# A transformer layer on one core: the side work of a pair moved behind the low parts of its activations

## The chip, the cores and the metric

The kernel runs on one core of a Trainium2 chip. The metric is the device time of one execution in microseconds (us), as the median of several runs. The engines are PE (TensorE, matmul) with its weight loads (PEld), DVE (VectorE), ACT (ScalarE), POOL (GpSimd) and SP (SyncE), which here issues all the DMAs.

## The reference, cut to what matters

One encoder layer is applied to 512 + 1024 tokens of width 1024, in float32:

```python
h = h + concat([attention(q, k, v), pooling(u)]) @ w_out
m = rmsnorm(h, norm_mlp_g)
h = h + square(relu(m @ w_up)) @ w_down          # the stage of this change; D_FF = 4096
gate = sigmoid(rmsnorm(h, norm_ple_g) @ w_ple_gate)
h = h + gate * (p_i @ w_ple_proj)
return rmsnorm(h, final_norm_g)
```

## The kernel before, in words

Every float32 operand of a matmul is split into a high part (a cast on ACT) and a low part (a subtraction on DVE or POOL); a product is three matmuls, high x high, high x low, low x high (`three`). The 1536 tokens are three chunks `c` of 512. A residual chunk `hT[c]` is four blocks of 128 x 2 x 512, each in one of 49 slots of one shared pool.

The stages follow each other: input projection (to about 190 us), attention with the output projection (to 579 us), the MLP (579 to 1625 us), the gated embedding and the last norm. PE, ACT, DVE and POOL execute in the order in which the program names the instructions. SP's order is chosen by a scheduler among what is ready; `load` adds that a load isn't put ahead of the last PE instruction named before it.

**The MLP.** For each chunk there are 16 pairs (`Pair(c, g)`), each of 256 of the 4096 hidden units. `run` computes the 2 x 2 blocks of a pair by seven products (Strassen's scheme) of 12 matmuls with 256 columns, in the order 1, 6, 2, 5, 7, 3, 4. Products 1 and 2 add up in one PSUM bank (`px`), 5 and 3 in another (`pz`), 7 and 4 in a third (`pq`); 6 has `py`. Between them stand the four down blocks of the pair before (`between(i)` calls `before.down(i)`): 12 matmuls with 512 columns into `pd`, whose sum DVE adds to `hT[c][i]` (L837). The order on PE is 1, down 0, 6, 2, down 1, 5, 7, down 2, 3, 4, down 3.

The tail of a pair makes its activations: ACT takes relu of c1 and of c2, the square as high part (L876, L882) and the exact square (L877, L883), and DVE the low parts (L886) into `r`. Down 0 of the next turn needs them.

**Side work.** After each product, `after(i)` issues one step of each of these: `feeding` (the sums and splits of the next pair's w_up, L786 to L804, and the load of w_up after that, `wur`), `splits` (w_down of this pair, L816 and L817), `raising` (L662, at the start of a chunk), and `step()`, one step of the queue `chores`. Chores are generators: `make_m` builds the normed inputs `mo_d` of a chunk, `spill` stores a residual chunk, `invert` and `finishing` belong to a chunk's end. `after(3)` and `after(4)` stand ahead of the low parts, so their instructions come first on DVE and ACT.

**The norm of the MLP.** The residual is multiplied with a per-token row w before the chunk's pairs add to it (`raise_h`: 8 operations on DVE). The end of `make_m(c)` computes w into `acc[:, 1]` (L646), stores it in `w_d[c]` (L647), and `load_ms(c)` loads it at the chunk's first pair.

**Start of the stage.** `heads_out(p)` gives eight pieces of the output projection for each 256 tokens; p = 5 are the last tokens of chunk 2. When they are through, `spill(2)` joins the chores, waits 16 steps and stores the four blocks of chunk 2 (L708). Meanwhile the 14 halves of `mo` for chunk 0 are loaded, then `h` of chunk 0, and `wur` of pair 1 by the fourth step of `feeding`.

Of the kernel before, what the change touches and what calls it, by code (L numbers as in the profile page):

```python
# [20 lines left out]
KD = D // P  # L21
# [14 lines left out]
def encoder_layer(ctx, tc, xT, xn, xr, pT, w1, w2, w_pool, w_out, w_up, w_down, w_gate, w_proj,  # L36
# [558 lines left out]
    def make_m(c, et, el):  # L595

        A, B = slice(0, HF), slice(HF, CH)
        acc = slot([P, 2, CH], F32, f"sqm{c}")  # L600

        def squares_of(b, m):
            for i in range(2):
                sq = slot([P, 2, CH], F32, f"sqm{c}{b}{i}")
                for h in range(2):
                    out = sq[:, h] if b + i + h else acc[:, 0]
                    yield ((lambda i=i, h=h, out=out: sc.activation(out, m[i][:, h], AF.Square)),
                           (lambda out=out, first=b + i + h == 0: None if first else
                            et.tensor_tensor(acc[:, 0], acc[:, 0], out, op=ALU.add)))

        for b in range(2):
            m = [slot([P, 2, CH], F32, f"m{c}_{2 * i + b}") for i in range(2)]
            for i in range(2):
                load(m[i], h_d[c][2 * i + b])
            yield from wait(5)
            yield from lagged(squares_of(b, m))
            for i in range(2):
                for h in range(2):
                    k = 2 * (2 * i + b) + h
                    sc.activation(m[i][:, h], m[i][:, h], AF.Copy, scale=gmlp_sb[:, k:k + 1])  # L620
                yield
            tt = [slot([P, 2, 2, HF], F32, f"t{c}_{b}{i}") for i in range(2)]
            t1, t2, t3, t4 = (tt[i // 2][:, i % 2] for i in range(4))
            b11, b12, b21, b22 = m[0][:, :, A], m[0][:, :, B], m[1][:, :, A], m[1][:, :, B]
            for o, x, y in ((t1, b12, b11), (t2, b22, t1), (t3, b22, b12), (t4, b21, t2)):
                et.tensor_tensor(o, x, y, op=ALU.subtract)
                yield

            def pairs():
                for i, x in ((1, b11), (6, t2), (2, b21), (5, t1), (7, t3), (3, b22), (4, t4)):  # L630
                    out = slot([P, 2, 2, HF], F32R, f"mm{c}_{i}{b}")

                    def low_part(i=i, x=x, out=out):
                        el.tensor_tensor(out[:, 1], x, as32(out[:, 0]), op=ALU.subtract)
                        for j in range(2):
                            sy.dma_start(mo_d[c][i][j][:, 2 * b:2 * b + 2], as32(out[:, j]))
                    yield (lambda x=x, out=out: sc.copy(out[:, 0], x)), low_part
            yield from lagged(pairs())
        sh = slot([P, 2, CH], F32R, f"sh{c}")
        sc.copy(sh[:, 0], acc[:, 0])  # L640
        el.tensor_tensor(sh[:, 1], acc[:, 0], as32(sh[:, 0]), op=ALU.subtract)
        yield from wait(7)
        bc = tp_ps(f"w{c}")
        for i in range(2):
            pe.matmul(bc, ones_sb, sh[:, i], start=i == 0, stop=i == 1)
        ve.tensor_scalar(acc[:, 1], bc, 1.0 / D, EPS, op0=ALU.mult, op1=ALU.add)  # L646
        sy.dma_start(w_d[c], acc[:, 1])  # L647

    def load_mo(c, i):
        MO[c, i] = [slot([P, 4, HF], F32R, f"mo{c}_{i}{j}") for j in range(2)]  # L650
# [52 lines left out]
    away = set()  # L703

    def spill(c):
        yield from wait(16 if c == 2 else 0)
        for a in range(4):
            sy.dma_start(h_d[c][a], hT[c][a])  # L708
        away.add(c)
        yield  # L710
# [30 lines left out]
    def heads_out(p):  # L741

        c, sl = p // 2, slice(p % 2 * 2 * P, (p % 2 + 1) * 2 * P)

        def piece(d):
            def go():
                assert c not in away
                h = hT[c][d // 2][:, d % 2, sl]
                po = (ps("pp", f"po{p}{d}") if prompt[0] else ps("s", f"po{p}{d}") if ending[0] and (p == 4 or d % 2)
                      else acc_ps("acc", f"po{p}{d}"))[:, 0:2 * P]  # L750
                for k in range(4):
                    ws = [w[:, d * P:(d + 1) * P] for w in WO[k]]
                    for i, (w_, x_) in enumerate(three(ws, [x[:, k, :] for x in cat[p]])):
                        pe.matmul(po, w_, x_, start=k == 0 and i == 0, stop=k == 3 and i == 2)
                ve.tensor_tensor(h, po, h, op=ALU.add)
                if d == KD - 1 and p % 2:
                    chores.append(spill(c))
                    if c == 0:
                        chores.append(make_m(0, gp, gp))
            return go  # L760
        return [piece(d) for d in range(KD)]


    class Pair:
# [62 lines left out]

        def down(self, a):
            pd = ps("d", f"pd{self.id}{a}")
            for e in range(2):  # L830
                d = 2 * a + e
                for f in range(2):
                    ws_ = [w[:, d * P:(d + 1) * P] for w in self.wd[f]]
                    for i, (w_, x_) in enumerate(three(ws_, [self.r[f][:, 0], self.r[f][:, 1]])):
                        pe.matmul(pd[:, e * CH:(e + 1) * CH], w_, x_, start=f == 0 and i == 0, stop=f == 1 and i == 2)
            h = hT[self.c][a]
            ve.tensor_tensor(h, pd.rearrange("p (a b) -> p a b", a=2), h, op=ALU.add)  # L837

        def run(self, between, after):

            A, B = slice(0, HF), slice(HF, CH)
            u = slot([P, 4, HF], F32, f"u{self.id}")
            t, u2, u4 = u[:, 0], u[:, 1], u[:, 2]
            c = slot([P, 2, CH], F32, f"c{self.id}")
            c1, c2 = c[:, 0], c[:, 1]
            self.r = [slot([P, 2, CH], F32R, f"r{self.id}{i}") for i in range(2)]

            def bank(tag, nm):
                return (tp_ps(f"{nm}{self.id}") if tag == "tp" else ps(tag, f"{nm}{self.id}"))[:, 0:HF]

            x = bank("tp", "px")
            self.product(1, x)
            sc.copy(t, x)
            after(1)
            between(0)
            y = bank("u", "py")
            self.product(6, y)
            ve.tensor_tensor(u2, y, t, op=ALU.add)
            after(6)
            self.product(2, x, False)  # L860
            sc.activation(c1[:, A], x, AF.Relu)
            after(2)
            between(1)
            z = bank("tp", "pz")
            self.product(5, z)
            ve.tensor_tensor(u4, z, u2, op=ALU.add)
            after(5)
            q = bank("u", "pq")
            self.product(7, q)
            ve.tensor_tensor(c2[:, B], q, u4, op=ALU.add)  # L870
            after(7)
            between(2)
            self.product(3, z, False)
            ve.tensor_tensor(c1[:, B], z, u2, op=ALU.add)
            sc.activation(c1[:, B], c1[:, B], AF.Relu)
            sc.activation(self.r[0][:, 0], c1, AF.Square)  # L876
            sc.activation(c1, c1, AF.Square)  # L877
            after(3)
            self.product(4, q, False)
            ve.tensor_tensor(c2[:, A], q, u2, op=ALU.add)  # L880
            sc.activation(c2, c2, AF.Relu)
            sc.activation(self.r[1][:, 0], c2, AF.Square)  # L882
            sc.activation(c2, c2, AF.Square)  # L883
            after(4)
            for i, x in enumerate((c1, c2)):
                ve.tensor_tensor(self.r[i][:, 1], x, as32(self.r[i][:, 0]), op=ALU.subtract)  # L886
            between(3)

    NG = NF // 2
    pairs = [Pair(c, g) for c in range(3) for g in range(NG)]  # L890

    def stream():

        for n, pr in enumerate(pairs):
            for i, _ in enumerate(pr.feed()):
                if i == 3 and n + 1 < len(pairs):
                    pairs[n + 1].load_up()
                yield
    feeding = stream()
# [167 lines left out]

    pairs[0].load_down()
    load_mo(0, ORDER[5]), load_mo(0, ORDER[6])
    for a in range(4):  # L1070
        load_h(0, a, h_d[0][a])
    while fill:
# [107 lines left out]
    for n, pair in enumerate(pairs):  # L1180
        c, g = pair.c, pair.g
        raising = None
        if g == 0:
            if c:
                for a in range(4):
                    load_h(c, a, h_d[c][a])
            load_ms(c)
            raising = raise_h(c)
        if g == 1:
            chores.append(invert(c))  # L1190
# [10 lines left out]
            if i == 1 and n + 1 < len(pairs):  # L1201
                pairs[n + 1].load_down()

        def after(i):
            next(feeding, None)
            next(splits, None)
            if raising:
                next(raising, None)
            if g == NG - 1 and c < 2:
                load_mo(c + 1, i)  # L1210
            if n == len(pairs) - 1:
                if i == 1:
                    chores.append(first_weights())
                if i in (5, 7, 3, 4):
                    load_in(0, (5, 7, 3, 4).index(i))
            step()

        pair.run(between, after)
        for _ in splits:
            pass  # L1220
        for _ in raising or ():
# [175 lines left out]
```

## Time and profile before

| what | us |
|---|---|
| median of 3 runs (1812.99 to 1815.73) | 1815.48 |
| the profiled execution, its own time | 1813.31 |
| its span | 1811.5 |
| PE busy | 1759.7 |
| DVE busy | 1260.0 |
| POOL busy | 1053.7 |
| ACT busy | 939.7 |

The granted clock of TensorE was 0.995 over the span; 256.84 MB were moved by DMA. In the rows of the profile a busy share is that of a span or window, a wait is put down to what ended it ("x <- y"), and L49 is the line of every matmul, so groups are told apart by the tiles' names: `pd` is a down block, `px`, `py`, `pz`, `pq` are products. Rows of a timeline give start, duration, engine, line, operation, and in brackets the idle time just before.

### The profile page before, as it was taken

The page shows a single profiled execution, that of the slowest core. Times are in us where ns is not written, and L with a number is a line of the kernel's source. Part 1 is how long each engine was busy: PE and PEld are TensorE (multiplying, and loading weights), DVE is VectorE, ACT ScalarE, POOL GpSimd, SP SyncE. Part 2 cuts the span into 40 slices and gives each one's busy share as a digit, 9 for nine tenths or more (in the row PEclk, how much of TensorE's full clock was granted, in tenths as well). Part 3 has the DMA queues.
Part 4 walks back from the last instruction along what each step waited for, and adds up shares of the span by engine and source line. Part 5 has one row for each costly group of instructions (what it writes and reads, how often), then busy time and mean ns, then how long its engine had stood idle before and what let it go on. Part 6 is the DMA issues. An engine that isn't in the chain of part 4 may idle for free.

```text
span 1811.5 us, 28604 instructions
## 1 busy us (share of the span) xinstructions
PE 1759.7 (97%) x10540; PEld 1537.1 (85%) x10540; DVE 1260.0 (70%) x1843; ACT 939.7 (52%) x1854; POOL 1053.7 (58%) x923
## 2 busy tenths in 40 slices
PE   9999899999999799999999999999999999999997
PEld 7888777888868798988888889889898999888887
DVE  5677865888894677865568877876776556665655
ACT  6434455768794455655445545554455444443332
POOL 3474774535674567676656776785577666543121
PEclk9999999999999899999999999999999999999998
DMA  6333545120519335343364442556443323272102
GB/s 248 114 123 105 216 165 185 36 94 13 206 46 367 139 122 198 121 177 100 136 265 157 163 151 96 195 185 235 179 157 100 110 94 99 89 262 70 59 12 82
DMA packets 83883, 256.84 MB, mean 142 GB/s; under 512 B 9888, under 2 KB 16416, under 8 KB 83744
## 3 DMA queue, kind: packets, MB, share of 16 engines
q1 hardware_dynamic: 83744, 255.02, 39.7%
q8 instruction: 83, 1.36, 0.3%
q14 instruction: 56, 0.46, 0.1%
HBM read 195.74 MB, written 59.24 MB: 141 GB/s over the span
## 4 chain that ended last, share of the span: by engine, by line
PE 78%; DVE 7%; ACT 5%; DMA 3%; issue 3%; POOL 1%; POOLq 0%; DVEq 0%; ACTq 0%; SPq 0%
PE pd L49 25%; PE z L49 7%; PE px L49 6%; PE pz L49 6%; PE pq L49 6%; PE pg L49 6%; PE py L49 4%; PE pp L49 3%; PE o L49 3%; PE tp L53 3%; PE po L49 3%; PE S L49 3%; PE pj L49 1%; DMA wur<-in_w_up_dram 1%; DVE r L886 1%
## 5 line engine op out<-in xcount | busy, mean ns | idle before, releaser
L49 PE MATMUL pd<-r,wd 128*128 128x512 f32 x2304 | 568.5, 395 | 10.8 <-DVE r L886 10.6
L49 PEld LDWEIGHTS pd<-r,wd 128*128 128x128 f32 x2304 | 419.5, 188 | 100.3 <-DVE r L886 16.1
L787 POOL TENSOR_TENSOR w<-ws,w 128x512 fp32r<-128x512 f32 x192 | 272.5, 1423 | 217.9 <-ACT w L786 206.8
L787 POOL TENSOR_TENSOR w<-wur,w 128x512 fp32r<-128x512 f32 x144 | 212.8, 1489 | 135.4 <-ACT w L786 134.4
L837 DVE TENSOR_TENSOR h<-pd,h 128x1024 f32<-128x1024 f32 x192 | 233.5, 1216 | 76.6 <-PE pd L49 76.5
L786 ACT CAST w<-ws 128x512 fp32r<-128x512 f32 x192 | 118.5, 617 | 271.1 <-DVE ws L795 241.1
L461 POOL TENSOR_SCALAR pr<-pr,rr 128x512 f32<-128x512 f32 x160 | 111.2, 705 | 134.7 <-DVE rr L456 66.8
L49 PE MATMUL z<-w,x 128*128 128x512 f32 (+1 forms) x864 | 175.7, 359 | 0.9 <-DVE w L160 0.5
L49 PEld LDWEIGHTS pz<-mo,w 128*128 128x128 f32 x1152 | 150.7, 190 | 19.3 <-issue 11.2
L49 PEld LDWEIGHTS z<-w,x 128*128 128x128 f32 x864 | 142.9, 189 | 28.0 <-ACT w L159 2.1
L49 PE MATMUL pz<-mo,w 128*128 128x256 f32 x1152 | 153.6, 283 | 10.2 <-issue 10.2
L817 DVE TENSOR_TENSOR wd<-wdr,wd 128x512 fp32r<-128x512 f32 x96 | 102.8, 1071 | 83.1 <-ACT wd L816 76.6
L49 PE MATMUL pq<-mo,w 128*128 128x256 f32 x1152 | 153.7, 283 | 1.0 <-issue 1.0
L49 PE MATMUL px<-mo,w 128*128 128x256 f32 x1152 | 152.2, 281 | 0.0
L49 PEld LDWEIGHTS px<-mo,w 128*128 128x128 f32 x1152 | 146.5, 189 | 4.0
L49 PEld LDWEIGHTS pq<-mo,w 128*128 128x128 f32 x1152 | 144.7, 191 | 1.4 <-issue 1.3
L49 PE MATMUL pg<-hg,wg 128*128 128x512 f32 (+1 forms) x768 | 141.0, 338 | 0.2
L472 ACT CAST pt<-tp 128x512 fp32r<-128x512 f32 x160 | 88.0, 591 | 88.5 <-PE tp L53 86.8
L49 PEld LDWEIGHTS pg<-hg,wg 128*128 128x128 f32 x768 | 118.6, 188 | 17.8 <-DVE hg L1128 1.0
L817 POOL TENSOR_TENSOR wd<-wdr,wd 128x512 fp32r<-128x512 f32 x96 | 131.8, 1373 | 2.6 <-DMA w_d<-sqm 2.6
L886 DVE TENSOR_TENSOR r<-c,r 128x512 fp32r<-128x512 f32 x96 | 74.7, 783 | 74.1 <-ACT c L883 46.2
L473 DVE TENSOR_TENSOR pt<-tp,pt 128x512 fp32r<-128x512 f32 x160 | 104.0, 684 | 31.4 <-ACT pt L472 31.1
(195 smaller groups left out, 3036.2 us busy)
## 6 DMA issues: line engine op xcount, KB each, us to landing
wur<-in_w_up_dram SPq DMA_DIRECT2D x96, 512.0 KB, 4.2
wdr<-in_w_down_dram SPq DMA_DIRECT2D x96, 512.0 KB, 4.4
mo_d<-mm SPq DMA_DIRECT2D x84, 256.0 KB, 2.3
mo<-mo_d SPq DMA_DIRECT2D x42, 512.0 KB, 7.7
h_d<-h SPq DMA_DIRECT2D x16, 512.0 KB, 3.0
h<-h_d SPq DMA_DIRECT2D x16, 512.0 KB, 9.9
xn<-in_xn_dram SPq DMA_DIRECT2D x12, 512.0 KB, 6.4
qs_d<-qs SPq DMA_DIRECT2D x12, 512.0 KB, 3.0
```

What stands on the lines that cost most here:

```text
L49: last_pe[0] = nc.tensor.matmul(*a, **k).ins
L53: last_pe[0] = nc.tensor.transpose(*a, **k).ins
L461: gp.tensor_scalar(p, p, rr, 1.0, op0=ALU.mult, op1=ALU.mult)
L472: sc.copy(self.pt[kt][:, 0], tp)
L473: ve.tensor_tensor(self.pt[kt][:, 1], tp, as32(self.pt[kt][:, 0]), op=ALU.subtract)
L786: sc.copy(t[:, 0], x)
L787: gp.tensor_tensor(t[:, 1], x, as32(t[:, 0]), op=ALU.subtract)
L817: (gp, ve)[i].tensor_tensor(lo, self.dr[i][:, h], as32(hi), op=ALU.subtract)
L837: ve.tensor_tensor(h, pd.rearrange("p (a b) -> p a b", a=2), h, op=ALU.add)
L886: ve.tensor_tensor(self.r[i][:, 1], x, as32(self.r[i][:, 0]), op=ALU.subtract)
```

## The change

1. `after(i)` is divided into `used(i)`, right after a product (loads that take the place of its input), and `hook()` (the side work). There are still seven hooks: after products 1, 6, 2, 5 and 7 as before, one behind both low parts, and one behind down 3.
2. A down block runs f (the half of the hidden units) outside and e (the half of the block's columns) inside, so the six matmuls with `r[1]` come last.
3. The row w of chunk 0 stays in `acc[:, 1]`; its store and load go. The raise of chunk 0 begins at the third hook and takes two steps in each.
4. The last chunk's residual is stored block by block by the pieces of p = 5, and `spill(2)` with its 16 waiting steps goes.
5. `wur` of pair 1 is loaded ahead of `h` of chunk 0; `feeding` loads from pair 2 on.

```diff
@@ end of make_m
-        sy.dma_start(w_d[c], acc[:, 1])
+        if c:
+            sy.dma_start(w_d[c], acc[:, 1])
+        else:
+            ws[0] = acc[:, 1]
@@ spill
-        yield from wait(16 if c == 2 else 0)
@@ heads_out
-                if d == KD - 1 and p % 2:
+                if p == 5:
+                    if d % 2:
+                        sy.dma_start(h_d[c][d // 2], hT[c][d // 2])
+                elif d == KD - 1 and p % 2:
@@ Pair.down
-            for e in range(2):
-                d = 2 * a + e
-                for f in range(2):
+            for f in range(2):
+                for e in range(2):
+                    d = 2 * a + e
@@ Pair.run (product(i) now calls used(i) behind the product)
             self.product(3, z, False)
 ...
-            sc.activation(self.r[0][:, 0], c1, AF.Square)
-            sc.activation(c1, c1, AF.Square)
-            after(3)
+            square(0, c1)
             self.product(4, q, False)
             ve.tensor_tensor(c2[:, A], q, u2, op=ALU.add)
             sc.activation(c2, c2, AF.Relu)
-            sc.activation(self.r[1][:, 0], c2, AF.Square)
-            sc.activation(c2, c2, AF.Square)
-            after(4)
-            for i, x in enumerate((c1, c2)):
-                ve.tensor_tensor(self.r[i][:, 1], x, as32(self.r[i][:, 0]), op=ALU.subtract)
+            square(1, c2)
+            low_part(0, c1)
+            low_part(1, c2)
+            hook()
             between(3)
+            hook()
@@ stream
-                if i == 3 and n + 1 < len(pairs):
+                if i == 3 and 0 < n < len(pairs) - 1:
                     pairs[n + 1].load_up()
@@ start of the stage
     load_mo(0, ORDER[5]), load_mo(0, ORDER[6])
+    pairs[1].load_up()
     for a in range(4):
         load_h(0, a, h_d[0][a])
@@ loop over the pairs
-            load_ms(c)
+                load_ms(c)               # inside "if c:"
-        def after(i):
+        hooks = itertools.count(1)
+        def hook():
             next(feeding, None)
             next(splits, None)
-            if raising:
+            for _ in range(0 if not raising else 1 if c else 2 if next(hooks) > 2 else 0):
                 next(raising, None)
+            step()
+        def used(i):
             if g == NG - 1 and c < 2:
                 load_mo(c + 1, i)
 ...
-            step()
```

More of the change, by code (lines that the diff above doesn't have):

```diff
@@ L1 @@
+import itertools
 import math
@@ L837, in down, with run @@
             ve.tensor_tensor(h, pd.rearrange("p (a b) -> p a b", a=2), h, op=ALU.add)
-        def run(self, between, after):
+        def run(self, between, used, hook):
             A, B = slice(0, HF), slice(HF, CH)
@@ L849, in bank, with product, square, low_part @@
                 return (tp_ps(f"{nm}{self.id}") if tag == "tp" else ps(tag, f"{nm}{self.id}"))[:, 0:HF]
+            def product(i, out, fresh=True):
+                self.product(i, out, fresh)
+                used(i)
+            def square(i, x):
+                sc.activation(self.r[i][:, 0], x, AF.Square)
+                sc.activation(x, x, AF.Square)
+            def low_part(i, x):
+                ve.tensor_tensor(self.r[i][:, 1], x, as32(self.r[i][:, 0]), op=ALU.subtract)
             x = bank("tp", "px")
-            self.product(1, x)
+            product(1, x)
@@ L853, in run @@
             sc.copy(t, x)
-            after(1)
+            hook()
             between(0)
             y = bank("u", "py")
-            self.product(6, y)
+            product(6, y)
             ve.tensor_tensor(u2, y, t, op=ALU.add)
-            after(6)
-            self.product(2, x, False)
+            hook()
+            product(2, x, False)
             sc.activation(c1[:, A], x, AF.Relu)
-            after(2)
+            hook()
             between(1)
             z = bank("tp", "pz")
-            self.product(5, z)
+            product(5, z)
@@ L866, in run @@
             ve.tensor_tensor(u4, z, u2, op=ALU.add)
-            after(5)
+            hook()
             q = bank("u", "pq")
-            self.product(7, q)
+            product(7, q)
             ve.tensor_tensor(c2[:, B], q, u4, op=ALU.add)
-            after(7)
+            hook()
             between(2)
-            self.product(3, z, False)
+            product(3, z, False)
             ve.tensor_tensor(c1[:, B], z, u2, op=ALU.add)
             sc.activation(c1[:, B], c1[:, B], AF.Relu)
-            sc.activation(self.r[0][:, 0], c1, AF.Square)
@@ L877, in run @@
-            sc.activation(c1, c1, AF.Square)
-            after(3)
-            self.product(4, q, False)
+            square(0, c1)
+            product(4, q, False)
             ve.tensor_tensor(c2[:, A], q, u2, op=ALU.add)
             sc.activation(c2, c2, AF.Relu)
-            sc.activation(self.r[1][:, 0], c2, AF.Square)
-            sc.activation(c2, c2, AF.Square)
-            after(4)
-            for i, x in enumerate((c1, c2)):
-                ve.tensor_tensor(self.r[i][:, 1], x, as32(self.r[i][:, 0]), op=ALU.subtract)
+            square(1, c2)
@@ L887, in run @@
+            low_part(0, c1)
+            low_part(1, c2)
+            hook()
             between(3)
+            hook()
     NG = NF // 2
@@ L1215, in after @@
                     load_in(0, (5, 7, 3, 4).index(i))
-            step()
-        pair.run(between, after)
+        pair.run(between, used, hook)
         for _ in splits:
```

## The prediction

> **What bounds the kernel now.** I read the page first, then the waits of PE, then the MLP stage (579 to 1625 us) pair by pair.
>
> ```profile
> PE 1759.7 (97%) x10540; PEld 1537.1 (85%) x10540; DVE 1260.0 (70%) x1843; ACT 939.7 (52%) x1854; POOL 1053.7 (58%) x923
> ...
> PE pd L49 <- DVE r L886: 10.6, 11, 1.8
> PE pz L49 <- issue: 10.2, 3, 9.2
> ...
> DVE h L662 <- DMA w<-w_d: 25.0, 3, 11.4
> ```
>
> TensorE (PE) is busy for 97% of the span, and no edit removes a product. So the change can only win or lose PE's waits. The waits give total us, times and the longest: 10.6 us on the low part of an activation (r, L886), and 9.2 us once on a product into pz. The third line is VectorE (DVE), which waited 11.4 us in one piece for the loaded row w.
>
> The windows below give span, busy us of PE, PEld, DVE, ACT and POOL, then the granted clock, DMA share and GB/s. The first is pair 0, the second pair 1, the third an undisturbed pair, the fourth the fullest of POOL.
>
> ```profile
> 579.01:600.74 21.73, 12.53 (x87) 12.36 (x86) 10.08 (x17) 7.21 (x15) 8.97 (x8) 0.77 0.82 330
> 600.74:624.85 24.11, 21.61 (x133) 18.91 (x133) 17.68 (x21) 11.86 (x23) 14.51 (x10) 1.00 0.25 88
> 815.98:837.07 21.09, 21.09 (x133) 19.00 (x132) 12.55 (x17) 10.41 (x20) 12.65 (x10) 1.00 0.30 100
> 688.15:709.29 21.14, 21.14 (x134) 19.02 (x132) 14.98 (x17) 13.19 (x26) 19.83 (x15) 1.00 0.49 177
> 580.00:590.00 10.00, 6.28 (x53) 6.08 (x52) 0.83 (x2) 3.86 (x8) 5.85 (x5) 1.00 1.03 413
> 590.00:600.00 10.00, 4.52 (x21) 4.55 (x22) 7.78 (x14) 2.64 (x5) 2.80 (x3) 0.53 0.65 263
> 600.00:610.00 10.00, 7.50 (x46) 6.35 (x46) 9.70 (x9) 5.56 (x12) 6.69 (x5) 0.96 0.33 105
> ```
>
> An undisturbed pair takes 21.09 us. Four products start between 579.01 and 584.71 below, 1.42 us each; that leaves (21.09 - 7 x 1.42) / 4 = 2.79 for a down block, 0.232 for each of its 12 matmuls. Pair 0 has no down blocks and should take 9.9 us; it took 21.73. Pair 1 lost 3.0. The start of the stage therefore holds 14.8 us, more than all other waits on r.
>
> ```profile
> 579.01 1.57 PE L49 MATMUL px<-mo,w 128*128 128x256 f32 x12
> 580.42 1.59 PE L49 MATMUL py<-mo,w 128*128 128x256 f32 x12
> ...
> 584.71 1.57 PE L49 MATMUL pq<-mo,w 128*128 128x256 f32 x12
> 595.48 2.90 PE L49 MATMUL pz<-mo,w 128*128 128x256 f32 x12 [9.20 <-issue]
> 598.18 2.76 PE L49 MATMUL pq<-mo,w 128*128 128x256 f32 x12
> ...
> 604.34 0.96 PE L49 MATMUL pd<-r,wd 128*128 128x512 f32 x3 [1.77 <-DVE r L886]
> 606.04 2.12 PE L49 MATMUL pd<-r,wd 128*128 128x512 f32 x8 [0.74 <-DVE r L886]
> 592.22 0.69 DVE L662 TENSOR_TENSOR h<-h,w 128x512 f32<-128x512 f32 x1 [11.38 <-DMA w<-w_d]
> 592.83 0.42 DVE L858 TENSOR_TENSOR u<-py,u 128x256 f32<-128x256 f32 x1
> ...
> 594.96 0.42 DVE L866 TENSOR_TENSOR u<-pz,u 128x256 f32<-128x256 f32 x1
> 585.45 1.27 POOL L817 TENSOR_TENSOR wd<-wdr,wd 128x512 fp32r<-128x512 f32 x1 [2.56 <-DMA w_d<-sqm]
> 575.93 0.32 SPq L647 DMA_DIRECT2D w_d<-sqm  x1
> ...
> 580.89 1.64 SPq L56 DMA_DIRECT2D wur<-in_w_up_dram  x2
> 585.38 0.33 SPq L56 DMA_DIRECT2D w<-w_d  x1
> ```
>
> This is the cause at the start. The first raise (L662) stands on DVE ahead of L858 and L866, and waits for a row stored at 575.93 and loaded again at 585.38. Product 3 adds into the bank that L866 reads, so it starts behind 594.96. After the idle time the clock is 0.53, and products 3 and 4 take 2.70 and 2.56 us by their starts, which is 2.4 too much.
>
> **The change, part by part.**
>
> *Row of chunk 0 kept in SBUF; raise from the third hook, two per hook.* The store, the load and the POOL wait on the store's slot (2.56 us) go. What is late next? I ran the four queues forward by hand. PE reaches 584.71 + 1.43 = 586.14 unhindered. The matrix `wur` of pair 1 now goes ahead of the four `h`, whose first is this:
>
> ```profile
> 569.53 11.30 DMA h<-h_d
> 605.91 1.77 DVE L662 TENSOR_TENSOR h<-h,w 128x512 f32<-128x512 f32 x1
> 607.60 1.77 DVE L804 TENSOR_TENSOR ws<-wur,ws 128x512 f32<-128x512 f32 x1
> ...
> 605.39 1.73 POOL L787 TENSOR_TENSOR w<-ws,w 128x512 fp32r<-128x512 f32 x1
> 607.09 1.73 POOL L817 TENSOR_TENSOR wd<-wdr,wd 128x512 fp32r<-128x512 f32 x1
> 586.68 1.26 POOL L787 TENSOR_TENSOR w<-ws,w 128x512 fp32r<-128x512 f32 x1
> ```
>
> It landed at 580.83. Two blocks of 512 KB at 413 GB/s take 2.5 us, so `h` lands from 583.4. SP issues the four block stores behind the `h` loads. Each waits for its piece's add on DVE; the last piece is done when px starts at 579.01, and `wdr` of pair 1 and `wur` of pair 2 queue behind. They are needed from about 596 and 603, so I charge nothing; without this cover each store holds them for one 1.3 us transfer.
>
> The price is in the other rows. Alone, DVE starts a two-input operation every 0.61 us (592.22 to 592.83) and POOL takes 1.26; side by side they take 1.77 and 1.73, that is, they alternate. From 581.5 POOL has six splits in hand. The moved raises must pass between them. Hook 3 issues one wd split and raises 0 and 1 ahead of L866: the alternation puts them at 585.4, 587.1 and 589.0, L866 ends at 590.0, and product 3 starts 3.9 us late. L870, behind four more operations, ends at 593.7 and holds product 4 for 2.2 us. Squares and low parts then end at 598.1 and 599.9, so the first down block of pair 1 ends at 601.2. Before, it ended at 606.04 + 2.12 = 608.15, so the gain is 7.0 us. Without any stall it would end at 579.01 + 8 x 1.42 + 2.79 = 593.2: the gain lies between 0 (the wait moves to a late `h` or a late slot, which the 2.5 us may also worsen) and 15.0. I take 7.0.
>
> For the alternation the Trainium skill has a rule (SBUF — State Buffer, "SBUF: two separate sides"): a DVE operation with two SBUF inputs and a GpSimd operation exclude each other for their whole length. The trace agrees by the 1.77 and 1.73. It speaks against the change, which puts eight raises beside the splits that were alone on DVE before. By the rule the sum stands as here, without it by rival 1.
>
> *Side work behind the low parts; f outside e in a down block.* In an undisturbed pair:
>
> ```profile
> 834.69 0.63 ACT L877 ACTIVATE c<-c 128x512 f32<-128x512 f32 x1
> 835.23 0.60 ACT L786 CAST w<-wur 128x512 fp32r<-128x512 f32 x1
> 835.74 0.62 ACT L881 ACTIVATE c<-c 128x512 f32<-128x512 f32 x1
> ...
> 837.84 0.69 DVE L886 TENSOR_TENSOR r<-c,r 128x512 fp32r<-128x512 f32 x1 [1.71 <-ACT c L883]
> 838.48 1.78 PE L49 MATMUL pd<-r,wd 128*128 128x512 f32 x7
> 1012.05 1.26 DVE L886 TENSOR_TENSOR r<-c,r 128x512 fp32r<-128x512 f32 x1 [1.68 <-ACT c L883]
> 1013.37 2.13 PE L49 MATMUL pd<-r,wd 128*128 128x512 f32 x8 [1.46 <-DVE r L886]
> ```
>
> The second low part ends at 838.53; the block starts at 838.48 and needs it at its fifth matmul, 838.48 + 4 x 0.232 = 839.4. With f outside it is the eighth, 0.70 us later. The copy at 835.23 goes behind the squares, which brings the low part 0.51 us forward. A disturbed pair also loses DVE's wait on POOL (1.26 against 0.69): 0.57. Together 1.2 to 1.8 us, against waits of 0.2 to 1.5. Besides the first pair (1.77 + 0.74), 10.6 - 2.5 = 8.1 us of them are left. If 1.2 us is all, some 0.9 us of the three longest (about 1.5 each) stays; I take 7.6, between 7.2 and 8.1.
>
> What queues behind instead: the next pair's splits 2 and 5 on ACT and POOL, DVE's s3 and s4, chores, and the load of the next `wur`, now traced behind the last down block. That matrix is first used at hook 4, 4 x 1.42 + 2 x 2.79 = 11.3 us on, and the slowest load shown took 11.30: 0.
>
> ```profile
> 835.98 1.30 POOL L787 TENSOR_TENSOR w<-wur,w 128x512 fp32r<-128x512 f32 x1 [3.90 <-ACT w L786]
> 821.58 1.60 PE L49 MATMUL px<-mo,w 128*128 128x256 f32 x12
> ```
>
> Product 2 starts 5.60 us after its pair (821.58 against 815.98), next at 842.67. Its split, on POOL from 835.98, would run at 837.8 to 839.1, with 3.6 us to spare: cost 0, and each further POOL operation takes 1.3 of it. L866 and L870 have one product and one block, 4.2 us, before PE needs their bank: 0.
>
> *Spill without its 16 waits.* Chores after it come two pairs earlier. The four reciprocals of `invert` then fall in pair 1, where DVE was idle for 24.11 - 17.68 = 6.4 us: 0, at most 1.9 if two of them delay L866. The bytes moved are the same. In chunks 1 and 2 row and `h` are still loaded (the rest of the 25.0 us): 0.
>
> **Sum.** 7.0 + 7.6 = 14.6 us off. The profiled execution took 1813.31 us (span 1811.5), 2.2 under the median 1815.48: 1798.7 beside it, 1801 as a median.
>
> **Rivals.**
> 1. Raises don't collide with POOL. With 0.61 us each, L866 ends at 587.1, product 3 waits 1.0, product 4 1.5 and the first block 1.7: 4.2 in place of 8.0 lost. Gain 10.8 + 8.1: 1796.6. For: 592 to 595, where DVE ran at 0.61. Against: POOL was idle there.
> 2. The clock falls again. The 3.9 us wait lies between one of 1.77 us (clock 0.96 in its window) and one of 9.20 (0.53); it is nearer to the first, so I charged nothing. If it falls, 2.4 us come back: 1803. The Trainium skill (TensorE: Matmul & The Clock Gate, "What's actually happening") has the half clock after an idle window of about 3.4 us; by that rule this rival holds, and these rows don't contradict it.
> 3. The start gains nothing: a wd tile gets a slot that a block store still reads, or `h` lands late, as DMA is full (share 1.03). Only 7.6: 1808.
> 4. Nothing measurable: as 3, and late splits (rival 5) take three quarters of the 7.6: 1814.
> 5. Slower: splits 2 and 5, now behind the squares, come late for product 2. It begins where over 3.6 us of POOL work stands ahead, near three operations. For: POOL was busy 19.83 of 21.14 us at 688. Against: the average pair has 12.65. At 0.6 us in each of 47 pairs, 28 us: 1829; it decides from 0.4 us per pair, which eats 18.
>
> **How the numbers follow.** Forecast 0.46, rival 1 0.17, rival 2 0.12, rival 3 0.08, rival 4 0.09, rival 5 0.08. What a measurement can tell from no change is about 0.2%, 3.6 us. Faster is 0.46 + 0.17 + 0.12 + 0.08 = 0.83, same 0.09, slower 0.08. The range goes from the full gain (15.0 + 8.1: 1792) to where nothing could be measured any more (1811), and leaves out rivals 4 and 5.
>
> **What would show it.** Right: no L662 that waits for w before 600; product 3 of pair 0 waits 3 to 5 us for L866; DVE raises of 1.2 to 1.8 us there; no wait on L886 above 0.4 us; pairs near 1009 and 1032 at 21.1 to 21.7 in place of 23. Wrong: a wait of product 2 on L787, L662 waiting for `h`, wd on a store, or half clock behind 590.

## The result and the profile after

The changed kernel takes 1838.33 us (median of 4 runs, 1835.4 to 1838.72), the kernel before 1815.61 beside it (1812.99 to 1816.92): the ratio is 1.0123, interval 1.0106 to 1.0141. Forecast were 1801 us and faster; it is slower by 22.7 us. The profiled span grew from 1811.5 to 1836.2 us.

From the page of the changed kernel and its waits (total us, times, longest). L50 is the line of every matmul now, L867 the low parts (L886 before), L888 the add that frees the bank of `pq` (L870 before), L864 the exact square, L843 the add of a down block.

```profile
PE 1770.4 (96%) x10540; PEld 1544.2 (84%) x10540; DVE 1307.5 (71%) x1843; ACT 942.7 (51%) x1854; POOL 1068.0 (58%) x923
...
PE pq L50 <- DVE c L888: 20.8, 12, 3.2
PE pz L50 <- issue: 6.2, 1, 6.2
PE pd L50 <- DVE r L867: 0.9, 2, 0.8
...
DVE r L867 <- ACT c L864: 98.0, 91, 2.8
...
DVE ws L799 <- POOL w L793: 9.9, 4, 4.5
```

The waits on the low parts are gone (10.6 to 0.9), the wait at the start is shorter (9.2 to 6.2), and there is a new one: product 4 waits 12 times for L888, 20.8 us in all. DVE now stands idle 98 us for ACT's squares, with nothing to do there (46.2 and 8.3 us, for the two squares, before). In the last line the first sum for the next weights (L799) waits on DVE for splits on POOL; before, the same line was:

```profile
DVE ws L793 <- POOL w L787: 0.4, 1, 0.4
```

Where the 24.7 us came from, by windows: the start (product 1 of pair 0 to product 6 of pair 1), then product 6 of pair 1 to that of pair 47. Of before:

```profile
579.01:607.99 28.98, 17.28 (x110) 15.97 (x109) 17.10 (x24) 11.52 (x22) 14.71 (x12) 0.82 0.73 283
607.99:1595.44 987.45, 977.47 (x6098) 875.66 (x6096) 687.29 (x873) 511.92 (x956) 652.65 (x464) 1.00 0.43 148
```

and of after:

```profile
581.47:605.41 23.94, 16.77 (x110) 15.34 (x109) 13.37 (x21) 10.38 (x20) 10.75 (x10) 0.86 0.83 324
605.41:1620.33 1014.92, 987.54 (x6098) 882.19 (x6096) 740.31 (x876) 515.42 (x956) 669.65 (x466) 0.99 0.41 144
```

The stage begins 2.5 us later (581.47 against 579.01). That isn't the change's: in the other kernels told of below it began between 578.13 and 581.86, in no order with what they change, and in two profiles of one of them at 578.38 and 581.80. The start is 5.0 us shorter. The 46 pairs are 27.5 us longer, by two parts that the rows separate: PE is idle 27.38 us in place of 9.98 (1014.92 - 987.54; 987.45 - 977.47), which makes 17.4, and the same matmuls keep it busy 10.1 us longer. DVE is busy 53 us longer with practically the same operations.

One pair in detail, at the end of chunk 0, where the chore `finishing` has most work for DVE and POOL. Of before, L870 with the product behind it, then POOL:

```profile
1027.18 0.41 DVE L870 TENSOR_TENSOR c<-pq,u 128x256 f32<-128x256 f32 x1
...
1028.07 1.59 PE L49 MATMUL pq<-mo,w 128*128 128x256 f32 x12
...
1010.23 1.30 POOL L787 TENSOR_TENSOR w<-wur,w 128x512 fp32r<-128x512 f32 x1 [3.02 <-ACT w L786]
1011.50 1.26 POOL L1147 TENSOR_TENSOR sqg<-sqg,sqg 128x512 f32<-128x512 f32 x1
1012.73 1.73 POOL L787 TENSOR_TENSOR w<-ws,w 128x512 fp32r<-128x512 f32 x1
```

and of after:

```profile
1021.60 0.69 DVE L867 TENSOR_TENSOR r<-c,r 128x512 fp32r<-128x512 f32 x1 [2.77 <-ACT c L864]
1023.45 0.69 DVE L867 TENSOR_TENSOR r<-c,r 128x512 fp32r<-128x512 f32 x1 [1.16 <-ACT c L864]
1025.79 1.78 DVE L810 TENSOR_TENSOR ws<-wur,ws 128x512 f32<-128x512 f32 x1
...
1038.49 1.75 DVE L823 TENSOR_TENSOR wd<-wdr,wd 128x512 fp32r<-128x512 f32 x1
1040.77 0.41 DVE L888 TENSOR_TENSOR c<-pq,u 128x256 f32<-128x256 f32 x1
...
1024.01 1.29 POOL L793 TENSOR_TENSOR w<-wur,w 128x512 fp32r<-128x512 f32 x1 [4.89 <-DMA hg_d<-hg]
1025.25 1.77 POOL L1164 TENSOR_TENSOR sqg<-sqg,sqg 128x512 f32<-128x512 f32 x1
...
1041.33 1.84 PE L50 MATMUL pq<-mo,w 128*128 128x256 f32 x12 [2.43 <-DVE c L888]
1042.96 4.35 PE L50 MATMUL pd<-r,wd 128*128 128x512 f32 x12
```

Before, POOL used the time in which DVE waited for the squares: the operation at 1010.23 ran there whole, the one at 1011.50 in part. After, DVE and POOL are idle side by side there (POOL 4.89 us, DVE 2.77 and 1.16), and then both have everything left to do. In windows, from the end of the second low part to the add on `pq`, before and after:

```profile
1013.24:1027.18 13.94, 13.81 (x85) 12.41 (x86) 13.69 (x14) 4.29 (x9) 12.27 (x8) 1.00 0.39 133
1024.06:1040.77 16.71, 14.40 (x90) 12.59 (x89) 16.71 (x15) 5.49 (x11) 15.64 (x10) 1.00 0.40 144
```

After has one DVE operation and two POOL operations more in this stretch, and DVE hasn't a gap in it. The stretch is 2.77 us longer, and product 4 waits 2.43. L810, a sum with two SBUF inputs, shows that DVE and POOL collide in most of the pairs (total us and mean ns in the stage, after, then L804 of before):

```profile
L810 DVE TENSOR_TENSOR ws<-wur,ws 128x512 f32<-128x512 f32 x47 | 71.2, 1516 | 0.0
L804 DVE TENSOR_TENSOR ws<-wur,ws 128x512 f32<-128x512 f32 x47 | 35.2, 749 | 0.0
```

The four waits of 3.25, 3.17, 2.97 and 2.19 us, more than half of the 20.8, lie in other pairs, in which POOL makes low parts for `make_m`, and there DVE isn't full. Between the second low part and L888 it was busy 10.1 to 11.0 us of 14.3 to 17.3, POOL 13.0 to 17.3. DVE stands in its order ahead of L888 and waits for POOL, above all before L799 (4.51 us ahead of the longest wait), or for an ACT copy that itself waited for POOL; L799 and the subtraction behind it then take 1.5 to 1.8 us each beside POOL.

In the `finishing` pair above, the down block behind the wait took 4.35 us in place of 2.95: the granted clock fell too. Two such windows of after:

```profile
1041.00:1048.00 7.00, 6.67 (x32) 5.81 (x33) 3.32 (x6) 6.00 (x10) 1.29 (x1) 0.76 0.57 189
1218.00:1228.00 10.00, 7.82 (x40) 6.67 (x39) 7.61 (x8) 4.91 (x10) 7.34 (x6) 0.83 0.79 272
```

### The profile page after: what moved, and what is told of

The parts are those of the page before. It is cut to its first block, busy times and chain, and to the rows that moved or that the text cites. A ratio compares the mean times of both kernels' runs of the same rounds, so it can differ in the third digit from the quotient of the medians.

```text
span 1836.2 us, 28610 instructions
## 1 busy us (share of the span) xinstructions
PE 1770.4 (96%) x10540; PEld 1544.2 (84%) x10540; DVE 1307.5 (71%) x1843; ACT 942.7 (51%) x1854; POOL 1068.0 (58%) x923
## 5 line engine op out<-in xcount | busy, mean ns | idle before, releaser
L50 PE MATMUL pd<-r,wd 128*128 128x512 f32 x2304 | 570.0, 396 | 1.3 <-DVE r L867 0.9
L50 PEld LDWEIGHTS pd<-r,wd 128*128 128x128 f32 x2304 | 423.4, 190 | 88.1 <-DVE r L867 3.5
L793 POOL TENSOR_TENSOR w<-ws,w 128x512 fp32r<-128x512 f32 x192 | 288.8, 1510 | 157.2 <-ACT w L792 146.4
L793 POOL TENSOR_TENSOR w<-wur,w 128x512 fp32r<-128x512 f32 x144 | 208.5, 1459 | 207.9 <-ACT w L792 173.2
L843 DVE TENSOR_TENSOR h<-pd,h 128x1024 f32<-128x1024 f32 x192 | 233.3, 1215 | 39.3 <-PE pd L50 38.4
L50 PE MATMUL pq<-mo,w 128*128 128x256 f32 x1152 | 156.4, 285 | 23.5 <-DVE c L888 20.8
L50 PE MATMUL z<-w,x 128*128 128x512 f32 (+1 forms) x864 | 175.1, 359 | 1.6 <-ACT w L160 0.6
L823 DVE TENSOR_TENSOR wd<-wdr,wd 128x512 fp32r<-128x512 f32 x96 | 110.9, 1155 | 80.9 <-ACT wd L822 68.8
L50 PEld LDWEIGHTS pq<-mo,w 128*128 128x128 f32 x1152 | 145.0, 191 | 27.3 <-issue 24.5
L50 PEld LDWEIGHTS z<-w,x 128*128 128x128 f32 x864 | 142.4, 188 | 28.6 <-ACT w L160 2.4
L50 PEld LDWEIGHTS pz<-mo,w 128*128 128x128 f32 x1152 | 150.7, 190 | 18.4 <-issue 10.4
L50 PE MATMUL pz<-mo,w 128*128 128x256 f32 x1152 | 154.5, 284 | 7.7 <-issue 6.2
L50 PE MATMUL px<-mo,w 128*128 128x256 f32 x1152 | 152.7, 282 | 1.2 <-ACT u L871 1.2
L50 PEld LDWEIGHTS px<-mo,w 128*128 128x128 f32 x1152 | 146.8, 189 | 5.6 <-ACT u L871 1.6
L867 DVE TENSOR_TENSOR r<-c,r 128x512 fp32r<-128x512 f32 x96 | 67.1, 699 | 104.9 <-ACT c L864 98.0
L50 PE MATMUL pg<-hg,wg 128*128 128x512 f32 (+1 forms) x768 | 141.5, 339 | 0.2
L823 POOL TENSOR_TENSOR wd<-wdr,wd 128x512 fp32r<-128x512 f32 x96 | 136.0, 1416 | 0.0
L50 PEld LDWEIGHTS pg<-hg,wg 128*128 128x128 f32 x768 | 119.1, 188 | 17.8 <-DVE hg L1145 1.0
```

The costliest lines, as they stand in the source:

```text
L50: last_pe[0] = nc.tensor.matmul(*a, **k).ins
L793: gp.tensor_tensor(t[:, 1], x, as32(t[:, 0]), op=ALU.subtract)
L823: (gp, ve)[i].tensor_tensor(lo, self.dr[i][:, h], as32(hi), op=ALU.subtract)
```

## The experiments

Times are medians, in us; ratios are to the kernel before, as it ran beside each (1814.57 to 1815.69), with their interval. "Idle" and "busy" are PE's between product 6 of pair 1 and that of pair 47, from one window row of each kernel.

| kernel | time | ratio | idle | busy |
|---|---|---|---|---|
| before | 1815.61 | 1 | 9.98 | 977.47 |
| after | 1838.33 | 1.0123 (1.0106 to 1.0141) | 27.38 | 987.54 |
| hooks only | 1838.01 | 1.0125 (1.0112 to 1.0139) | 25.07 | 987.00 |
| hooks back | 1805.03 | 0.9949 (0.9935 to 0.9962) | 4.00 | 977.52 |
| f outside only | 1808.13 | 0.9961 (0.9947 to 0.9974) | 4.16 | 977.39 |
| hooks and spill back | 1806.21 | 0.9950 (0.9938 to 0.9963) | 3.86 | 977.12 |
| no POOL chores | 1809.44 | 0.9972 (0.9960 to 0.9983) | 8.02 | 980.14 |
| no DVE chores | 1802.01 | 0.9933 (0.9918 to 0.9948) | 4.27 | 977.24 |
| one hook back | 1825.25 | 1.0056 (1.0043 to 1.0070) | 19.39 | 982.75 |
| chores back | 1825.75 | 1.0059 (1.0045 to 1.0072) | 19.73 | 985.13 |
| splits back | 1823.37 | 1.0047 (1.0033 to 1.0061) | 16.30 | 984.04 |
| stores late | 1802.45 | 0.9933 (0.9921 to 0.9946) | 3.80 | 976.62 |
| stores late, again | 1802.79 | 0.9932 (0.9919 to 0.9944) | 3.86 | 976.61 |
| stores late, hook between | 1806.36 | 0.9951 (0.9937 to 0.9964) | 7.75 | 977.36 |

**Which part costs.** Theory A: side work that runs behind the squares stacks up on DVE and POOL and reaches L888. Rival B: the chores, 16 steps earlier by the missing wait of `spill`, meet in worse pairs. First the kernel before with nothing but the two hooks moved, then the kernel after with the hooks put back:

```diff
-            after(3)                                  # hooks only (in before)
-            after(4)
             ... both low parts
+            hook()
             between(3)
+            hook()
```

> The kernel before with one edit: the two hooks behind products 3 and 4 moved behind the low parts and behind down 3. Theory A (bunching: POOL has no side work while ACT makes the squares and gets it all afterwards; DVE then alternates with POOL and the sum L870 comes late for product 4): this edit alone carries the loss of 27 us between pairs 1 and 47, so 1835 to 1845 us, with waits of product 4 (pq) on L870 of 15 to 25 us in all. Rival B (the chores of chunk 0, 18 steps earlier without the waiting spill, collide): the hooks gain what the prediction said, 1806 to 1810, and no wait on L870.

```diff
             square(0, c1)                             # hooks back (in after)
+            hook()
             product(4, q, False)
 ...
             square(1, c2)
+            hook()
             low_part(0, c1)
             low_part(1, c2)
-            hook()
             between(3)
-            hook()
```

> The changed kernel with the two hooks put back ahead of the low parts; everything else of the change stays. Theory A: the start's gain of 5 us and the gain of f outside remain, 1803 to 1809 us, and no long wait of product 4. Rival B: as the changed kernel, 1832 to 1842.

The first took 1838.01, the second 1805.03. PE's waits, one row of each:

```profile
PE pq L50 <- DVE c L883: 14.1, 10, 2.6
...
PE pd L50 <- DVE r L867: 5.5, 5, 2.5
```

The moved hooks carry the whole loss; rival B falls, since hooks back has the earlier chores and loses nothing. The 14.1 us is a little under the 15 that theory A had. The rest of the change gains 10 where the hooks stand at their old places, and nothing beside the moved ones (1838.01 and 1838.33).

**What the rest is worth.** f outside e in a down block alone, in the kernel before; and hooks back with the old `spill` and its 16 waits:

```diff
-            for e in range(2):                        # f outside only (in before)
-                d = 2 * a + e
-                for f in range(2):
+            for f in range(2):
+                for e in range(2):
+                    d = 2 * a + e
```

> The kernel before with f outside e in the down blocks alone. By the matmul count the low part of r[1] is needed 0.70 us later, so of each wait on L886 up to 0.70 us goes: 5 to 6 us off, 1809 to 1811, and the longest such wait falls from 1.8 to about 1.1 (first pair) and 0.8. Rival: the order makes no difference because PE's own pace sets the pair, 1815.

```diff
     def spill(c):                                     # hooks and spill back (in after)
+        yield from wait(16 if c == 2 else 0)
@@ heads_out
-                if p == 5:
-                    if d % 2:
-                        sy.dma_start(h_d[c][d // 2], hT[c][d // 2])
-                elif d == KD - 1 and p % 2:
+                if d == KD - 1 and p % 2:
```

> As x2, with the last residual stored by the spill that waits 16 steps, as before. Slot theory (in the changed kernel ACT waits 4.1 us at the start for a wd slot that a block store still reads): that wait goes or gets shorter and the stage starts 2 to 4 us better than in x2. Rival: the slot is then that of another transfer and nothing changes against x2 (within 2 us).

f outside alone took 7.0 us off, a little more than expected, which is most of what the prediction hoped for from it and the moved copy together (7.6). The waits on the low parts fell from 10.6 to 5.3 us; the longest, in the first pair, stayed at 1.8, where 1.1 was expected. Storing block by block is worth nothing that these runs tell (1806.21 against 1805.03, the ranges overlap). The expectation for the start failed here: with the old spill ACT's third copy still waits 4.16 us for a block store.

**Which engine, and how much of the work.** Chores of one engine left out, then one of the two hooks back, then only the chores, or only the splits and sums, of both hooks back:

```diff
-                        el.tensor_tensor(out[:, 1], x, as32(out[:, 0]), op=ALU.subtract)   # no POOL chores (in after)
+                        if not c:
+                            el.tensor_tensor(out[:, 1], x, as32(out[:, 0]), op=ALU.subtract)
 ...
-                gp.tensor_tensor(acc[:, e], acc[:, e], sq[:, e], op=ALU.add)
```

> The changed kernel without POOL's part of the chores of chunks 1 and 2: make_m leaves out the low parts of its outputs (the high part is stored in their place) and finishing leaves out its sums of squares. DVE's chores stay. Theory A1 (POOL idles behind products 3 and 4, gets its work bunched, and holds DVE by the alternation and by slots that it frees late): waits of product 4 on L888 fall from 20.8 to under 6 us, 1812 to 1822 us. Theory A2 (DVE alone: it stands idle for the squares ahead of the side work and then lacks that time): above 1830, and the waits stay over 14 us.

```diff
-                ve.tensor_tensor(h[:, e], h[:, e], ws[c], op=ALU.mult)   # no DVE chores (in after)
 ...
-                    gate_in(0, a, False, (e,))
 ...
-                et.tensor_tensor(o, x, y, op=ALU.subtract)
+                if not c:
+                    et.tensor_tensor(o, x, y, op=ALU.subtract)
 ...
```

> The changed kernel without DVE's part of those chores: make_m leaves out its sums and differences, finishing the product with the row and the low parts of the gate's input. POOL's chores stay. A2: the waits of product 4 go, below 1818 us. A1: pairs 4, 7, 8 and 26, in which POOL makes the low parts of make_m, keep waits of 2 to 3 us each; those of pairs 19 to 21 go; 1820 to 1828.

```diff
             square(0, c1)                             # one hook back (in after)
+            hook()
             product(4, q, False)
 ...
             low_part(1, c2)
             hook()
             between(3)
-            hook()
```

> The changed kernel with the first of the two hooks put back behind the squares of product 3, the second behind both low parts. If the loss goes with the number of hooks moved, half of it stays: 1815 to 1825. If it comes from the POOL work of one hook, which starts only behind ACT's squares (the idle time of POOL ahead of split 2), the first hook carries it and this kernel is near 1803 to 1808, at or under the version with both hooks back (1805).

```diff
             square(0, c1)                             # chores back; splits back has "s" and "c" exchanged
+            hook("c")                                 # "c": step() alone
             product(4, q, False)
 ...
             square(1, c2)
+            hook("c")
             low_part(0, c1)
             low_part(1, c2)
-            hook()
+            hook("s")                                 # "s": feeding, splits and raise
             between(3)
-            hook()
+            hook("s")
```

> The kernel after, in which only the steps of the chores of the two moved hooks go back to their old places (behind the squares of c1 and of c2, ahead of the low parts); the steps of feeding and splits stay behind the low parts and behind down 3. Theory A (what counts is the sum of two-input operations of DVE and of POOL that stands behind the squares, of whatever kind): taking the chores out of it removes a part of the loss, as taking the chores of one engine out altogether did, so 1806 to 1825, waits of pq on the sum of DVE under 12 us. Rival C (it is the splits and sums of the next weights that come too late; the chores only happen to stand there): 1832 to 1840, waits as after, 18 us and more.

> The kernel after, in which only the steps of feeding and splits of the two moved hooks go back to their old places, and the chores stay behind the low parts and behind down 3. Theory A: 1806 to 1825, as in the kernel with the chores put back, since each takes a part out of the bunch; the losses of the two together make about the 33 us between hooks moved and hooks back. Rival C: 1803 to 1808, no wait of pq on DVE over 0.8 us.

PE's waits on L888 (its line differs by a few from kernel to kernel): no POOL chores, no DVE chores, one hook back, chores back, splits back.

```profile
PE pq L50 <- DVE c L889: 4.3, 7, 0.8
...
PE pq L50 <- DVE c L891: 2.8, 4, 0.8
...
PE pq L50 <- DVE c L888: 9.7, 11, 2.4
...
PE pq L50 <- DVE c L888: 15.6, 12, 2.9
...
PE pd L50 <- DVE r L867: 11.7, 7, 4.0
PE pq L50 <- DVE c L888: 6.6, 8, 1.4
```

Without the chores of either engine no wait on L888 is above 0.8 us, although hooks and splits stand where after has them; the sum that collides still does, and costs nothing (no DVE chores):

```profile
L813 DVE TENSOR_TENSOR ws<-wur,ws 128x512 f32<-128x512 f32 x47 | 82.3, 1751 | 0.0
```

So neither engine is the culprit by itself. Neither theory about one engine came out. 1809.44 lies under the range of A1; 1802.01 fits A2, but A2 gave over 1830 for the kernel without POOL's chores. What decides is when DVE reaches L888, and both queues behind the low parts set that: DVE's own work, slowed by turns with POOL, and POOL's splits, for which DVE waits. POOL's work alone doesn't do it: without DVE's chores, DVE's first sum waits for POOL's splits 1.6 us in all, against 9.9, with all of POOL's chores in place. How much of the loss comes by the turns and how much by the waits for POOL, these runs don't separate.

With half of the moved steps back, whichever half, 18 to 21 of the 33.3 us between after and hooks back remain (20.2, 20.7, 18.3): theory A's order of size, two of them just over the upper end of 1825, and not additive (20.7 + 18.3 is more than 33.3). Rival C, that the splits alone are late, falls: it gave 1832 to 1840 for chores back and 1803 to 1808 for splits back. In splits back part of the loss is another one, waits on the low parts of up to 4.0 us. Ahead of that wait a sum for the next weights, which stands before the low parts again, is held by POOL:

```profile
759.89 1.68 DVE L807 TENSOR_TENSOR ws<-wur,wur 128x512 f32<-128x512 f32 x1 [5.59 <-POOL w L793]
```

**The start.** In after, ACT's third copy into `wd` waits for a slot that a block store still reads, and DVE's raise and L884 stand behind it:

```profile
590.90 0.62 ACT L822 CAST wd<-wdr 128x512 fp32r<-128x512 f32 x1 [4.08 <-DMA h_d<-h]
591.55 0.69 DVE L823 TENSOR_TENSOR wd<-wdr,wd 128x512 fp32r<-128x512 f32 x1 [6.54 <-ACT wd L822]
592.16 2.37 DVE L666 TENSOR_TENSOR h<-h,sqm 128x512 f32<-128x512 f32 x2
594.45 0.41 DVE L884 TENSOR_TENSOR u<-pz,u 128x256 f32<-128x256 f32 x1
594.97 2.90 PE L50 MATMUL pz<-mo,w 128*128 128x256 f32 x12 [6.22 <-issue]
```

The start was tested in a kernel with hooks and spill back in which the stores of chunk 2 are also held, on SP, behind the loads of pair 2:

```diff
-            sy.dma_start(h_d[c][a], hT[c][a])         # stores late
+            ins = sy.dma_start(h_d[c][a], hT[c][a]).ins
+            if c == 2:
+                tc.add_manual_dep(ins, last_pe[0].name, NOSYNC, ...)
```

> The version with both hooks back and the old spill, with the four stores of chunk 2 held back on SP until after the loads of pair 2. Slot theory for the start: ACT's 4.2 us wait ahead of the third wd copy was for a slot that these stores still read, so it goes; product 3 of pair 0 then waits 1 to 4 us in place of 6.3, 1800 to 1804 us. Rival: the copy gets another slot as late, or its matrix is late, and nothing changes: 1805 to 1808.

It took 1802.45: the third copy doesn't wait any more, and product 3 waits 3.5 us. So the stores held the slot. The second profile of this kernel, from its run below:

```profile
588.72 3.42 DVE L666 TENSOR_TENSOR h<-h,sqm 128x512 f32<-128x512 f32 x2
592.06 0.41 DVE L884 TENSOR_TENSOR u<-pz,u 128x256 f32<-128x256 f32 x1
581.80 1.58 PE L50 MATMUL px<-mo,w 128*128 128x256 f32 x12
...
592.57 2.62 PE L50 MATMUL pz<-mo,w 128*128 128x256 f32 x12 [3.50 <-issue]
596.06 2.90 PE L50 MATMUL pq<-mo,w 128*128 128x256 f32 x12 [0.87 <-issue]
598.76 2.02 PE L50 MATMUL px<-mo,w 128*128 128x256 f32 x12
600.61 0.39 PE L50 MATMUL pd<-r,wd 128*128 128x512 f32 x1
602.72 2.82 PE L50 MATMUL pd<-r,wd 128*128 128x512 f32 x11 [1.72 <-DVE r L867]
605.38 1.60 PE L50 MATMUL py<-mo,w 128*128 128x256 f32 x12
```

**The last place for the later hook.** In the kernel with late stores that hook was put between the two low parts, and run beside the kernel itself:

```diff
             low_part(0, c1)
+            hook()
             low_part(1, c2)
-            hook()    # ahead of low_part(0)
```

> The kernel with both hooks at their old places and the stores of chunk 2 held behind the loads of pair 2, in which the later hook (behind the square of c2) now stands between the low part of c1 and that of c2. The first low part then no longer stands behind a hook on DVE, and the second, which f outside needs 0.7 us later, does. Theory: the waits of pd on a low part (6.0 us, 5 times, there) shrink by 2 to 4 us, 1798 to 1802. Rival: the hook ahead of the first low part was never what made it late (ACT's squares were), so the same time, 1802 to 1804; or the second low part is now late in place of the first, 1804 to 1808.

> The same kernel as the one with both hooks back and the stores held, run again beside the one with the later hook between the low parts, so that the two can be compared on one chip: 1801 to 1804 by its earlier runs.

1806.36 against 1802.79. The waits on the low parts are 7.2 us in 7 places, against 4.9 in 5. In all seven it is the second low part that is late, as the rival had it; without the move it was the second in four places, with 3.2 us. Hooks back with late stores is the fastest of the kernels that leave nothing out, 0.7% under before (0.9932, 0.9919 to 0.9944).

## Why the prediction was wrong, step by step

- **"L866 and L870 have one product and one block, 4.2 us, before PE needs their bank: 0."** This step failed, and with it the sum. The 4.2 us is the time between two products; it is cover only if DVE comes to the add at once. In the full pair of before the add ends at 1027.18 + 0.41 = 1027.59 and product 4 starts at 1028.07: 0.48 us were left, and the trace of before held these rows. In that pair the moved steps brought one DVE and two POOL operations behind the low parts, the stretch grew by 2.77 us, and product 4 waited 2.43. In the pairs of the longest waits DVE came late because it waited for POOL and then ran in turns with it. In all, the term put at 0 became 20.8 us of waits on L888, and the 46 pairs 27.5 us longer.
- **"What queues behind instead ... 0", by average.** Rival 5 was weighed by the average pair (POOL 12.65 of 21 us). The loss stands in the pairs with chores: 12 waits make 20.8 us, most pairs have none. Rival 5 had the sign and the cause, work that stands behind the squares. Its size came out by luck: the 0.6 us a pair was assumed for the split of product 2, and 27.5 us over 46 pairs happens to be 0.6 too. The place was L888 and product 4, and product 2 never waits for a split; product 4 does, 1.7 us in three places.
- **Alternation.** The prediction charged it at the start, and in a disturbed pair for the low part alone. At the start two raises took 3.42 us together (with late stores, beside a busy POOL), near the 1.77 quoted. The trace agrees with the rule named there (the Trainium skill, SBUF — State Buffer, "SBUF: two separate sides"). The turns show in the other pairs too, and the prediction left them out of the work that it put behind the low parts: L810 went from 749 to 1516 ns by its new place.
- **Waits on L886, 7.6.** Right: 10.6 went to 0.9 us in after, all of it in the first pair. f outside brings most of the time (7.0 us alone); the moved hooks can add at most the 4 us of idle time that hooks back still has.
- **The start, 7.0.** 5.0 in after. No raise waits for w there. Product 3 waited 6.22, not 3.9: rival 3's mechanism (a slot that a block store reads) held, at part of its price. With the stores late the wait is 3.50, and the add for product 3 ends 592.06 + 0.41 - 581.80 = 10.7 us after product 1, where the hand simulation had 590.0 - 579.01 = 11.0. The 2.2 us for product 4 was 0.87. But the first down block, with a wait of 1.72 us on its low part, ended 605.38 - 581.80 = 23.6 us after product 1, not 22.2. The three waits are 6.1 us, less than the 8.0 forecast; the clock, in the next point, costs more than that saves.
- **The clock, rival 2.** "I charged nothing" was wrong. The starts 592.57, 596.06, 598.76 and 600.61 (the block behind) make three products of 8.04 - 0.87 = 7.17 us, 2.9 over 3 x 1.42; rival 2 had 2.4. In the two other profiles with a wait of 3.50 us there the same sum gives 1.7 (stores late, first run) and 3.9 (hook between), so one wait has no fixed price. These waits agree with the rule of an idle window of about 3.4 us (the Trainium skill, TensorE: Matmul & The Clock Gate, "What's actually happening"). The shorter ones in the last section don't: the clock fell after 2.19 and 2.43 us as well.
- **Spill without waits, 0.** Held.

## What to carry to other kernels

Before moving side work, read in the trace the slack of every operation that frees a bank or a slot behind its new place, in the fullest repetition of the loop and not in the average one: here it was 0.48 us where the count of products said 4.2. An engine's idle time in front of a result that is late anyway (here DVE's and POOL's behind the squares) is a cheap place for side work. Here, taking the work out of there saved less than it then cost elsewhere (hooks moved against hooks back: 33 us), with two engines whose operations took turns and waited for one another. Changing the order in which the consumer uses late results (f outside) took half of the waits away, and 7.0 us off the time, without moving any work.

## What the runs showed of the hardware

The length of a wait didn't decide alone whether the clock fell. In after the longest wait on L888 was followed by a product and a block at full speed:

```profile
685.87 1.66 PE L50 MATMUL pq<-mo,w 128*128 128x256 f32 x12 [3.25 <-DVE c L888]
687.36 2.97 PE L50 MATMUL pd<-r,wd 128*128 128x512 f32 x12
...
1222.16 1.78 PE L50 MATMUL pq<-mo,w 128*128 128x256 f32 x12 [2.19 <-DVE c L888]
1223.74 4.41 PE L50 MATMUL pd<-r,wd 128*128 128x512 f32 x12
```

The shorter waits of 2.19 and, in the pair above, 2.43 us were followed, a product later, by blocks of 4.41 and 4.35 us. Over the pairs PE's busy time grew with its idle time: 977 us where 4 to 10 us were idle (980.14 in one kernel), 982.75 to 987.54 where it was 16 to 27. From before to after, 17.4 us more of idle time thus came with 27.5 us more in all, 1.6 times as much. The two blocks quoted hold 2.9 of the 10.1 us; the rest lies in smaller pieces, and which waits bring it stays open.
